# The last eight steps of FF2: the squares of a finished pair of tiles made one step later, behind GpSimd's second weight sum

## The chip, the cores and the metric

One core of one Trainium2 chip runs the whole kernel. The metric is the device time of one execution in microseconds (us). The kernel before takes 2620.69 us, the median of 3 runs (2619.88 to 2621.56).

Engines are named as in the profile: PE (TensorE, matmuls), DVE (VectorE), ACT (ScalarE), POOL (GpSimd), SP (the queue that issues most DMAs). L199 is line 199 of the kernel.

## The reference, cut to what matters

The kernel computes one layer of an encoder for 640 tokens of width 2048. The change lies in its last part, the down projection of the feed-forward block and the final norm:

```
x = x + (silu(h @ w_gate) * (h @ w_up)) @ w_down        # h = RMSNorm(x); w_down is 5632 x 2048
y = x * rsqrt(mean(x * x, axis=-1) + 1e-6) * norm_final
```

The mean of squares is taken over all 2048 columns of x, so every finished output tile of the down projection (128 columns by 640 tokens) gives its squares to one running sum.

## The kernel before

FF2, the down projection, runs as 32 steps. A step takes one pair q of output tiles (columns q and q + 8 of the 16 tiles) and some 5 or 6 blocks of the inner dimension; pair q has steps q, q + 8, q + 16 and q + 24, so that the last eight steps (24 to 31) each finish a pair. Each step multiplies 2 x 2 blocks with seven products instead of eight. The products run in the order p1, p6, p7, p2, p5, p4, p3 (`quartet`, L916), and with five blocks each is 15 matmuls of 128x128 by 128x320: for each block one with the weight's high half and the activation's high half (L207), one with the high half and the low half (L208), and one with the weight's low half (L209). Steps 30 and 31 are cut in two: an early part (p1, p6, p7, p5, p4) of both and then a late part (p2, p3).

Around a product stand these instructions:

- SP loads four weight blocks for a step (L936: b12, b22, b11, b21, in this order). They go through six buffers, and a load waits until its buffer's last reader is done. The load of b22 for the next step takes the buffer of this step's b12, which p7's weight split reads last.
- DVE makes b12 - b22 (L949) and s6 = b11 - that (L951) for the next step, in the middle of this one.
- POOL makes b22 - s6 into b11 (L954, the weights of p5) and b21 - s6 into b21 (L963, the weights of p4). L963 overwrites what p2 reads, so it waits for p2's split.
- ACT writes the high half of a product's weights (L198) and DVE the low half (L199), both 128x640. The pair of buffers is that of the product three before.
- DVE adds each finished product from PSUM to the tiles of the pair (L973, 128x320); after p6, in the last eight steps, three more adds read SBUF alone.
- POOL loads the activations of a coming step (L980).

The engines work in the order in which a scheduler has put their instructions; a wait at the head of one holds all that stands behind it on that engine.

The squares: `add_square` (L274) has ACT square a tile of 128x640 (L280; L277 for the very first, which starts the sum) and POOL add it to the running sum `ssq` (L281). In the kernel before, the loop over steps 0 to 29 calls it after the whole of a step t >= 24, twice, for the two tiles of the pair. The functions `squares` and `finish` do the same for the last two pairs and write the output; they are not changed. `n.later` is a list of stretches of the program; `keep_behind` (L155) ties each ACT, DVE and POOL instruction of such a stretch to the instruction of its engine that was emitted last ahead of the stretch, so that the scheduler cannot pull it forward past that one.

Of the kernel before, what the change touches and what calls it, by code (L numbers as in the profile page):

```python
# [29 lines left out]
STEPS = 32  # L30
# [3 lines left out]
def active(step):  # L34

    return [j for j in range(NPAIR) if (step - START[j]) % STEPS < 8]
# [13 lines left out]
class Net:  # L50
# [20 lines left out]
    def add(self, queue, work):  # L71
        self.queues.setdefault(queue, []).append(work)
# [230 lines left out]
def build(nc, tc, io, pools):  # L303
    n = Net(nc, tc, io, pools)
# [526 lines left out]
    r_b, ssq = n.get("S"), n.get("S")  # L831
# [169 lines left out]
    def fetch_late():  # L1001
        for which in late:
            for j in active(0):
                if j not in raw_pairs:
                    fetch(j, which)
        late.clear()

    def split_raws():
        at = n.emitted()
        which, own = raws.pop(0)  # L1010
        for j, k, raw in own:
            for a in range(k):
                t = n.get("S")
                hi, lo = hl = pack(t, HT)
                part = raw[:, a * HT:a * HT + HT]
                nc.scalar.activation(hi, part, AF.Identity)
                (nc.vector, nc.gpsimd)[a].tensor_tensor(lo, part, f(hi), ALU.subtract)
                lefts[j + a][which] = t, hl
            n.put("S", raw)
        n.later.append((at, n.emitted()))  # L1020

    def keep_last(which):

        at = n.emitted()
        t = n.get("S")
        hi, lo = hl = pack(t, HT)
        nc.scalar.activation(hi, kept[which], AF.Identity)  # L1027
        (nc.vector, nc.gpsimd)[which % 2].tensor_tensor(lo, kept.pop(which), f(hi), ALU.subtract)
        lefts[NPAIR - 1][which] = t, hl
        if not kept:  # L1030
            n.put("S", *kept_own)
        n.later.append((at, n.emitted()))
# [83 lines left out]
    def fetch_waiting(left):  # L1116
        while len(waiting) > left:
            for j, which in waiting.pop(0):
                fetch(j, which)

    def step(t, part="all"):
        now = active(t)
        nxt = active(t + 1) if t + 1 < STEPS else []
        cnt, q, last = len(now), t % 8, t >= STEPS - 8

        def after(which):
            gone = [j for j in now if j not in nxt]
            n.put("S", *(lefts[j][which][0] for j in gone))
            if t == 0:
                fetch_late()  # L1130
                if which in (1, 2):
                    split_raws()
                for x in {0: (0,), 2: (1,), 4: (2,), 3: (4,), 5: (3,), 6: (5, 6)}.get(which, ()):
                    keep_last(x)
            waiting.append([(j, which) for j in nxt if j not in now and j != NPAIR - 1])
            fetch_waiting(2)

        if t < 8:
            x, y = n.get("S"), n.get("S")
            dma(out=x, in_=x2_d[q])  # L1140
            dma(out=y, in_=x2_d[q + 8])
            sums.append((x, y, n.get("S") if q % 2 == 0 else sums[-1][2]))
        x, y, u = sums[q]
        c11, c21, c12, c22 = x[:, :HT], x[:, HT:], y[:, :HT], y[:, HT:]
        us = u[:, HT * (q % 2):HT * (q % 2) + HT]
        o = 2 * sum(len(active(i)) for i in range(q, t, 8))
        load = lambda z: io["w_down"][q + 8 * (z % 2), :, o + cnt * (z // 2):o + cnt * (z // 2) + cnt]
        for name, bank in quartet(cnt, load, [lefts[j] for j in now], None, after, part):
            if name == "p1":
                if t < 8:  # L1150
                    nc.scalar.activation(us, bank, AF.Identity)
                else:
                    add(us, us, bank)
                add(c11, c11, bank)
            elif name == "p6":
                add(us, us, bank)
                if last:
                    for c in (c21, c22, c12):
                        add(c, c, us)
            elif name == "p7":  # L1160
                add(c21, c21, bank)
                add(c22, c22, bank)
            elif name == "p5":
                add(c22, c22, bank)
                add(c12, c12, bank)
            elif name == "p2":
                add(c11, c11, bank)
            elif name == "p4":
                add(c21, c21, bank)
            elif name == "p3":  # L1170
                add(c12, c12, bank)
            yield name

    def run(*args):
        for _ in step(*args):
            pass

    for t in range(STEPS - 2):
        run(t)
        if t >= STEPS - 8:  # L1180
            if t == STEPS - 8:
                ssq = n.get("S")
            for i in range(2):
                n.add_square(ssq, sums[t % 8][i], t == STEPS - 8 and i == 0, "S")


    r_y = n.get("S")

    def squares(q, half):
        h = slice(half * HT, half * HT + HT)  # L1190
        t = n.get("S")
        for i in range(2):
            nc.scalar.activation(t[:, i * HT:i * HT + HT], sums[q][i][:, h], AF.Square)
        if q == 6:
            for i in range(2):
                nc.vector.tensor_tensor(ssq[:, h], ssq[:, h], t[:, i * HT:i * HT + HT], ALU.add)
        n.put("S", t)
        return n.rstd_steps({half: [ssq[:, h], t[:, :HT], t[:, HT:]]}, D, None) if q == 7 else None
# [10 lines left out]
                nc.vector.scalar_tensor_tensor(t, t, gain, n.spread[half], ALU.mult, ALU.mult)  # L1209
            (nc.scalar if half == 0 and i % 2 else nc.sync).dma_start(out=io["o_y"][:, m, h], in_=t)  # L1210

    run(STEPS - 2, "early")
    squares(6, 1)
    run(STEPS - 1, "early")
    norm = squares(7, 1)
# [10 lines left out]
    at = n.emitted()  # L1226
# [99 lines left out]
```

## Time and profile before

| what | us |
|---|---|
| median of 3 runs | 2620.69 |
| the profiled execution | 2621.49 |
| its span, first to last instruction | 2619.7 |
| PE busy in the span | 2565.2 |
| DVE busy in the span | 2027.7 |
| POOL busy in the span | 663.8 |

The profiled execution is 0.8 us above the median of the runs. The times of single instructions below count from the start of the span. Steps 25 to 29, in which the kernel makes squares beside full steps, lie between 2482 and 2567 us.

### The profile page before, as it was taken

Reading aid. Unit: us, or ns where it says so; the run is one execution under the profiler, and the core shown is the slowest. Engines: PE = TensorE matmul, PEld = TensorE weight load, DVE = VectorE, ACT = ScalarE, POOL = GpSimd, SP = SyncE. Lnnn points to the kernel's source line nnn. Section 1 sums busy time; section 2 is a strip of 40 time slices with the busy share of each in tenths; the row PEclk is TensorE's granted clock in tenths of the full one; section 3 lists DMA queues with packets and bytes.
Section 4 is the critical chain, followed back from the end, with each engine's and each line's share of the span. In section 5 each row is a group of like instructions: output and inputs, shape, how many; then the busy total and the mean of one; then the engine's idle time right before and its main releaser. Section 6 shows DMA issues by size and latency. Waiting matters only on the chain.

```text
span 2619.7 us, 45100 instructions
## 1 busy us (share of the span) xinstructions
PE 2565.2 (98%) x17437; PEld 2527.9 (96%) x17437; DVE 2027.7 (77%) x3133; ACT 1101.9 (42%) x1797; POOL 663.8 (25%) x573
## 2 busy tenths in 40 slices
PE   8999999999999999999999999999999899999997
PEld 8999998999899999999999999999999899999996
DVE  5775676766866888788888888888888877777797
ACT  5553444444633644443433333433434333333343
POOL 0000000000301203332333333323324433333353
PEclk9999999999999999999999999999999999999998
DMA  5322232444655433443343343343445865666655
GB/s 172 101 69 91 94 102 86 133 124 130 214 188 185 155 131 122 160 162 126 131 142 126 130 144 123 131 146 120 133 147 176 280 189 157 175 175 169 192 156 176
DMA packets 178678, 383.87 MB, mean 147 GB/s; under 512 B 21856, under 2 KB 74080, under 8 KB 178464
## 3 DMA queue, kind: packets, MB, share of 16 engines
q1 hardware_dynamic: 154128, 326.92, 38.8%
q0 software_dynamic: 23184, 52.77, 7.1%
q8 instruction: 137, 2.24, 0.3%
q10 hardware_dynamic: 1152, 1.31, 0.1%
q14 instruction: 77, 0.63, 0.1%
HBM read 299.61 MB, written 80.58 MB: 145 GB/s over the span
## 4 chain that ended last, share of the span: by engine, by line
PE 85%; DVE 8%; DMA 3%; ACT 2%; issue 2%; POOL 0%; SPq 0%; DVEq 0%; ACTq 0%; POOLq 0%
PE dn L209 18%; PE dn L207 18%; PE dn L208 18%; PE at L207 9%; PE at L208 9%; PE at L209 9%; DVE W L199 2%; PE at L324 2%; DMA W<-w_down 1%; PE at L419 1%; DVE S L973 1%; ACT W L198 1%; PE at L215 1%; PE at L214 1%; ACT S L440 0%
## 5 line engine op out<-in xcount | busy, mean ns | idle before, releaser
L207 PE MATMUL dn<-S,W 128*128 128x320 f32 x3694 | 1152.5, 312 | 5.2 <-ACT S L1027 2.7
L209 PE MATMUL dn<-S,W 128*128 128x320 f32 x3694 | 1144.5, 310 | 6.7 <-DVE W L199 6.3
L208 PE MATMUL dn<-S,W 128*128 128x320 f32 x3694 | 1143.3, 310 | 2.0 <-DVE S L203 1.7
L198 ACT ACTIVATE W<-W 128x1024 fp32r<-128x1024 f32 (+2 forms) x632 | 608.2, 963 | 965.9 <-PE dn L208 542.8
L199 DVE TENSOR_TENSOR W<-W,W 128x1024 fp32r<-128x1024 f32 (+2 forms) x632 | 738.7, 1169 | 81.5 <-ACT W L198 77.6
L209 PEld LDWEIGHTS dn<-S,W 128*128 128x128 f32 x3694 | 694.1, 188 | 10.5 <-DVE W L199 10.1
L207 PEld LDWEIGHTS dn<-S,W 128*128 128x128 f32 x3694 | 694.7, 188 | 9.0 <-ACT S L1027 3.0
L208 PEld LDWEIGHTS dn<-S,W 128*128 128x128 f32 x3694 | 694.4, 188 | 4.1 <-DVE S L203 1.9
L209 PE MATMUL at<-S,W 128*128 128x320 f32 x1594 | 493.5, 310 | 4.9 <-DVE W L199 4.8
L207 PE MATMUL at<-S,W 128*128 128x320 f32 x1594 | 492.8, 309 | 0.5 <-ACT W L198 0.5
L208 PE MATMUL at<-S,W 128*128 128x320 f32 x1594 | 492.5, 309 | 0.0
L954 POOL TENSOR_TENSOR W<-W,W 128x1024 f32<-128x1024 f32 (+2 forms) x75 | 158.9, 2118 | 637.5 <-DVE W L199 453.6
L209 PEld LDWEIGHTS at<-S,W 128*128 128x128 f32 x1594 | 299.2, 188 | 7.3 <-DVE W L199 7.3
L207 PEld LDWEIGHTS at<-S,W 128*128 128x128 f32 x1594 | 299.3, 188 | 0.8 <-ACT W L198 0.8
L208 PEld LDWEIGHTS at<-S,W 128*128 128x128 f32 x1594 | 299.3, 188 | 0.0
L973 DVE TENSOR_TENSOR S<-S,dn 128x320 f32<-128x320 f32 x358 | 163.8, 480 | 65.4 <-PE dn L209 65.0
L963 POOL TENSOR_TENSOR W<-W,W 128x1024 f32<-128x1024 f32 (+2 forms) x75 | 163.6, 2181 | 118.9 <-DVE W L199 113.5
L949 DVE TENSOR_TENSOR W<-W,W 128x1024 f32<-128x1024 f32 (+2 forms) x76 | 124.6, 1640 | 62.8 <-DMA W<-w_down 29.5
L973 DVE TENSOR_TENSOR S<-S,at 128x320 f32<-128x320 f32 x262 | 123.3, 480 | 51.4 <-PE at L209 50.5
L980 POOL DMA_DIRECT2D S<-act_d x161 | 88.0, 547 | 178.6 <-PE dn L209 92.0
L951 DVE TENSOR_TENSOR W<-W,W 128x1024 f32<-128x1024 f32 (+2 forms) x76 | 83.4, 1097 | 61.6 <-DMA W<-w_up 31.4
L1044 DVE TENSOR_TENSOR S<-S,half 128x320 fp32r<-128x320 f32 x147 | 120.0, 837 | 1.9
(162 smaller groups left out, 2223.3 us busy)
## 6 DMA issues: line engine op xcount, KB each, us to landing
S<-act_d POOLq DMA_DIRECT2D x161, 320.0 KB, 3.7
W<-w_gate SPq DMA_DIRECT2D x88, 512.0 KB
W<-w_up SPq DMA_DIRECT2D x88, 512.0 KB
W<-w_in SPq DMA_DIRECT2D x66, 512.0 KB
W<-w_down SPq DMA_DIRECT2D x64, 384.0 KB
act_d<-half SPq DMA_DIRECT2D x147, 160.0 KB
act_d<-S SPq DMA_DIRECT2D x147, 160.0 KB
W<-w_down SPq DMA_DIRECT2D x68, 320.0 KB
```

The costliest lines, as they stand in the source:

```text
L198: self.nc.scalar.activation(hi, src, AF.Identity)
L199: self.nc.vector.tensor_tensor(lo, src, f(hi), ALU.subtract)
L207: mm(out, a[0], b[0], start=first, stop=False)
L208: mm(out, a[0], b[1], start=False, stop=False)
L209: mm(out, a[1], b[0], start=False, stop=last)
L949: nc.vector.tensor_tensor(b12[:, w], b12[:, w], b22[:, w], sub)
L951: nc.vector.tensor_tensor(s6[:, w], b11[:, w], b12[:, w], sub)
L954: eng.tensor_tensor(b11[:, w], b22[:, w], s6[:, w], sub)
L963: eng.tensor_tensor(b21[:, w], b21[:, w], s6[:, w], sub)
L973: add = lambda o, a, b: nc.vector.tensor_tensor(o, a, b, ALU.add)
L980: nc.gpsimd.dma_start(out=r(sh(t, 2, HT)), in_=r(act_d[which, :, j]))
L1044: nc.vector.tensor_tensor(r(src), src, hi, ALU.subtract)
```

## The change

The call of `add_square` moves from the end of step t into step t + 1, to the place where the generator of that step has just handed over product p5; `late_squares` also marks the stretch in `n.later`. For step 29 the place is p5 of the early part of step 30. The sums, their order and the tiles are the same.

```
+    ssq = None
+
+    def late_squares(t):
+
+        nonlocal ssq
         if t >= STEPS - 8:
             if t == STEPS - 8:
                 ssq = n.get("S")
+            at = n.emitted()
             for i in range(2):
                 n.add_square(ssq, sums[t % 8][i], t == STEPS - 8 and i == 0, "S")
+            n.later.append((at, n.emitted()))
+
+    for t in range(STEPS - 2):
+        for name in step(t):
+            if name == "p5":
+                late_squares(t - 1)
...
-    run(STEPS - 2, "early")
+    for name in step(STEPS - 2, "early"):
+        if name == "p5":
+            late_squares(STEPS - 3)
```

On DVE, PE and SP the order of the instructions stays as it was. On POOL and ACT it changes. The rows below are from step 28, in which the squares of step 27's pair are made; steps 26, 27 and 29 are alike but for the places of single loads L980. Names are buffers: W weights, S activations and tiles, numbers tell them apart.

POOL before, from the first weight sum of step 28 (L954) to that of step 29:

```order
L954 TENSOR_TENSOR W_4121_27114<-W_4120_27112,W_4122_27117 128x640
L281 TENSOR_TENSOR S_4023_26565<-S_4023_26565,S_4115_27102 128x640
L980 DMA S_4163_27384<-act_d 128x640
L980 DMA S_4166_27407<-act_d 128x640
L281 TENSOR_TENSOR S_4023_26565<-S_4023_26565,S_4116_27105 128x640
L980 DMA S_4170_27431<-act_d 128x640
L963 TENSOR_TENSOR W_4132_27190<-W_4132_27190,W_4122_27117 128x640
L954 TENSOR_TENSOR W_4149_27288<-W_4148_27286,W_4150_27291 128x640
```

POOL now, the same stretch:

```order
L954 TENSOR_TENSOR W_4119_27108<-W_4118_27106,W_4120_27111 128x640
L963 TENSOR_TENSOR W_4130_27184<-W_4130_27184,W_4120_27111 128x640
L281 TENSOR_TENSOR S_4044_26692<-S_4044_26692,S_4136_27229 128x640
L281 TENSOR_TENSOR S_4044_26692<-S_4044_26692,S_4137_27232 128x640
L980 DMA S_4170_27431<-act_d 128x640
L954 TENSOR_TENSOR W_4147_27282<-W_4146_27280,W_4148_27285 128x640
```

Both sums of squares (L281) have moved from between the two weight sums to behind the second one (L963).

ACT before, from the split of p1's weights in step 28 to that of p4's (the rows L198 are p1, p6, p7, p2, p5, p4):

```order
L198 ACTIVATE W_4123_27119<-W_4121_27114 128x640
L198 ACTIVATE W_4126_27143<-W_4122_27117 128x640
L280 ACTIVATE S_4115_27102<-S_3371_22438 128x640
L198 ACTIVATE W_4130_27169<-W_4119_27110 128x640
L280 ACTIVATE S_4116_27105<-S_3372_22439 128x640
L198 ACTIVATE W_4134_27193<-W_4132_27190 128x640
L198 ACTIVATE W_4136_27214<-W_4121_27114 128x640
L198 ACTIVATE W_4139_27236<-W_4132_27190 128x640
```

ACT now, the same stretch:

```order
L198 ACTIVATE W_4121_27113<-W_4119_27108 128x640
L198 ACTIVATE W_4124_27137<-W_4120_27111 128x640
L198 ACTIVATE W_4128_27163<-W_4117_27104 128x640
L198 ACTIVATE W_4132_27187<-W_4130_27184 128x640
L198 ACTIVATE W_4134_27208<-W_4119_27108 128x640
L280 ACTIVATE S_4136_27229<-S_3371_22438 128x640
L280 ACTIVATE S_4137_27232<-S_3372_22439 128x640
L198 ACTIVATE W_4139_27236<-W_4130_27184 128x640
```

The two squares (L280) have moved from ahead of p7's and p2's splits to behind p5's split and ahead of p4's.

## Rows read from the trace of the kernel before

**Rows 1.** PE's waits from 2484 to 2590: total us, times, longest us.

```profile
PE dn L209 <- DVE W L199: 4.9, 5, 1.8
PE at L209 <- DVE W L199: 1.7, 5, 0.6
```

**Rows 2.** Stretches from p7 to p7: length, busy PE, PEld, DVE, ACT, POOL, PEclk, DMA, GB/s.

```profile
2486.60:2502.00 15.40, 15.40 (x107) 15.40 (x106) 14.48 (x22) 7.55 (x11) 6.99 (x5) 1.00 0.36 91
2502.00:2518.00 16.00, 15.72 (x108) 15.41 (x106) 14.64 (x22) 7.46 (x11) 9.38 (x12) 1.00 0.76 223
2518.00:2534.70 16.70, 15.98 (x108) 15.46 (x107) 15.23 (x24) 6.43 (x9) 9.37 (x10) 1.00 0.60 161
2534.70:2551.50 16.80, 15.83 (x106) 15.31 (x105) 15.27 (x22) 7.42 (x11) 8.06 (x7) 1.00 0.45 134
2551.50:2569.40 17.90, 15.94 (x107) 15.41 (x106) 15.11 (x23) 7.43 (x11) 9.29 (x9) 1.00 0.63 170
```

**Rows 3.** Chain that ended last, 2484 to 2590: start, us, what.

```profile
2533.91 4.04 DMA W<-w_down
...
2550.82 5.14 DMA W<-w_down
...
2574.86 5.12 DMA W<-w_down
2580.18 2.63 POOL W L963
```

**Rows 4.** Timeline of DVE, 2519 to 2541: start, us, group [idle before <-releaser].

```profile
2521.23 0.87 DVE L949 TENSOR_TENSOR W<-W,W 128x640 f32<-128x640 f32 x1 [1.47 <-DMA W<-w_down]
...
2522.42 0.81 DVE L199 TENSOR_TENSOR W<-W,W 128x640 fp32r<-128x640 f32 x1
2523.16 1.28 DVE L973 TENSOR_TENSOR S<-S,S 128x320 f32<-128x320 f32 x3
...
2525.16 0.82 DVE L199 TENSOR_TENSOR W<-W,W 128x640 fp32r<-128x640 f32 x1
...
2529.69 2.07 DVE L199 TENSOR_TENSOR W<-W,W 128x640 fp32r<-128x640 f32 x1
2531.68 0.47 DVE L973 TENSOR_TENSOR S<-S,dn 128x320 f32<-128x320 f32 x1
2532.08 1.80 DVE L199 TENSOR_TENSOR W<-W,W 128x640 fp32r<-128x640 f32 x1
...
2537.98 1.03 DVE L949 TENSOR_TENSOR W<-W,W 128x640 f32<-128x640 f32 x1 [1.44 <-DMA W<-w_down]
```

**Rows 5.** Timeline of POOL, the same stretch.

```profile
2529.51 1.57 POOL L954 TENSOR_TENSOR W<-W,W 128x640 f32<-128x640 f32 x1 [1.35 <-DVE W L199]
2531.05 2.15 POOL L281 TENSOR_TENSOR S<-S,S 128x640 f32<-128x640 f32 x1
...
2534.26 1.59 POOL L281 TENSOR_TENSOR S<-S,S 128x640 f32<-128x640 f32 x1
...
2536.74 1.58 POOL L963 TENSOR_TENSOR W<-W,W 128x640 f32<-128x640 f32 x1
```

**Rows 6.** Timeline of ACT, 2500 to 2506 and 2519 to 2541.

```profile
2502.13 0.74 ACT L198 ACTIVATE W<-W 128x640 fp32r<-128x640 f32 x1 [1.52 <-PE dn L208]
...
2529.80 0.74 ACT L280 ACTIVATE S<-S 128x640 f32<-128x640 f32 x1 [0.91 <-DVE S L973]
```

**Rows 7.** Timelines of DVE and POOL elsewhere: 824 to 832, 1500 to 1506.

```profile
823.82 5.84 DVE L203 SCALAR_TENSOR_TENSOR S<-S,gains,S 128x640 fp32r<-128x640 f32 x3 [0.52 <-ACT S L202]
...
823.15 7.94 POOL L281 TENSOR_TENSOR S<-S,S 128x640 f32<-128x640 f32 x4 [25.57 <-ACT S L280]
...
1501.61 3.10 DVE L1044 TENSOR_TENSOR S<-S,half 128x320 fp32r<-128x320 f32 x2
...
1501.76 2.60 POOL L963 TENSOR_TENSOR W<-W,W 128x1024 f32<-128x1024 f32 x1 [1.56 <-DVE W L199]
```

**Rows 8.** Timeline of DVE, 2554 to 2575.

```profile
2572.88 0.82 DVE L949 TENSOR_TENSOR W<-W,W 128x640 f32<-128x640 f32 x1 [2.04 <-DMA W<-w_down]
```

More of the change, by code (lines that the diff above doesn't have):

```diff
@@ L1176, in run @@
             pass
-    for t in range(STEPS - 2):
-        run(t)
+    ssq = None
+    def late_squares(t):
+        nonlocal ssq
         if t >= STEPS - 8:
```

## The prediction

> **What bounds the kernel now.** I read the waits of PE first, in the steps that the change touches: from 2484 to 2590 PE waits 6.6 us, ten times, always for the low half of a product's weights that DVE makes (L199) [rows 1]. That is all that a change here can win. The stretches from one p7 to the next show what a step pays: a step of five blocks has 105 matmuls and takes 15.4 us where PE never waits (the first stretch, granted clock 1.00); steps 26 to 29 take 16.0, 16.7, 16.8 and 17.9, which is 0.6 + 1.3 + 1.4 + 2.5 = 5.8 us over [rows 2]. Step 25, before any pair of square sums, has no wait.
>
> Then the chain that ended last: it doesn't run through PE there but round a loop of DVE and a weight load. L949 of a step waits for the load of b22 (it stands idle 1.44 to 1.47 us before it) [rows 4]; DVE then works without a pause from L949 to the low half of the next p7 (2521.23 to 2533.88, 12.65 us); that split frees the buffer for the next load, issued at 2533.91, 4.04 us [rows 3], and the next L949 starts at 2537.98 [rows 4]. One turn is 16.75 us, against PE's 15.4.
>
> What lengthens the turn is POOL. A low half alone takes 0.81 us; the one at 2529.69 takes 2.07 and ends 0.68 after POOL's L954 (2529.51 + 1.57 = 2531.08), the one at 2532.08 takes 1.80 and ends 0.68 after the sum L281 (2531.05 + 2.15 = 2533.20) [rows 4, 5]. The sum in turn starts only when the first of these ends, 2531.76, and ends 1.44 later. So a POOL sum and a DVE instruction with two SBUF inputs go one after the other, whoever comes first; when both have more to do they alternate: elsewhere four L281 took 7.94 and three L203 between them 5.84, 1.95 to 1.99 each [rows 7]. The small adds obey too: two L1044 of 128x320 took 3.10 us around one POOL sum, while three free adds of that size take 1.28 [rows 4, 7]. An add from PSUM (2531.68, 0.47 us) does not wait, though a sum is running [rows 4, 5].
>
> **What it removes.** In before the first L281 holds up p7's low half by 1.80 - 0.81 = 1.0 us, inside the turn. The second (2534.26) meets only p2's low half, which ends before the load has landed, so it costs the turn next to nothing. Without both, the turn is 11.65 + 4.1 = 15.7 us, nearly PE's own. The squares on ACT ahead of p7's split go as well; ACT is half idle, so moving them costs nothing there, as long as p4's high half is ready in time (below).
>
> **What it adds.** I count from T, the start of p7 on PE. ACT splits p5 at T + 0.1 (L198 released by the end of p6) [rows 6] for 0.74; then the squares follow, 0.74 each [rows 6], done at 1.6 and 2.4. p4's high half comes at about 3 and is needed at 6.6: hidden. On POOL, L963 waits for p2's low half and fills 0 to 1.55; the sums queue behind it. The load of b22 lands at about 2.2: p7's low half ended 0.8 us ahead of T in before (2533.88 against 2534.7 [rows 2, 4]) and now ends 1.8 ahead, by what was removed; 4.0 on top.
>
> - First sum: 1.7 to 3.25. L949 is ready at 2.2 and gets its turn after it: done at 3.25 + 0.7 = 3.95, as if it had started at 3.1.
> - Second sum: ready since 3.25, takes its turn behind L949, done 1.44 later, 5.4. p5's low half, ready at 4.25, is held to 5.4 + 0.7 = 6.1 instead of 5.1: 1.0 us lost.
> - In before p4's low half ends 4.7 after L949's start (2521.23 to 2525.98, less 0.05 by which L949 was stretched) [rows 4]. Now: 3.1 + 4.7 + 1.0 = 8.8.
> - PE wants p5's low half at 4.7 and p4's at 6.9 (two products of 2.2, three of 2.2, and two matmuls of 0.15). It waits 1.4 at p5 and 0.5 at p4, and each restart costs 0.1: 2.15 us a step.
>
> If L949 came before the first sum, the second would meet the three S,S adds instead, and p4's half would end at the same 8.8. Both sums now lie in the stretch in which DVE has no pause, and the way PE - ACT - POOL - DVE - PE is longer than a step can hide. DMAs: the loads L980 that stand between the sums read buffers that PE has already left; each takes POOL 0.55 us. SP's queue isn't passed by anything.
>
> **The sum.** Step 25 (one sum only, held against the three adds): 0.5. Step 26, where an L980 stands ahead of the first sum, which pushes it to 2.1: 2.5. Steps 27 and 28: 2.15 each. Step 29, whose b22 took 5.14 [rows 3]: between 2.15 and 2.5, say 2.3. Together 9.6 against 5.8: +3.8. In step 30 L949 now starts at 3.5 after T [rows 8] in a gap of POOL; both sums then stand in front of it (1.7 to 4.8), which holds it 1.3 us; p4's half, the load that it releases (2574.86) and L963 behind that load, the end of the chain [rows 3], shift with it: +1.3. In all +5.1 us: 2621.49, the profiled execution, becomes 2626.6. That execution lies 0.8 above the median of the runs, so against the median: 2625.8.
>
> **Bounds.** A sum costs at least nothing (in a pause or beside PSUM adds) and at most 1.57 + what alternation adds. With the load at 5.14 in every step and the L980 always between the sums, a step pays 2.5 and step 30 0.5 more: +7.5, 2628.2.
>
> **Rivals.** (1) Faster: the sums don't hold DVE. Then the turn is 15.7 us, PE pays 0.3 a step instead of 1.45, 4 x 1.15 = 4.6 is won, and p7's earlier split gives step 30 some 0.4: 2615.7. It decides if DVE's instructions at 2 to 6 us after T run at 0.81 beside a sum. Against it stand the stretched instructions of rows 4 and 7 [rows 4, 7]. The Trainium skill (Advanced Engine Details and Errata, VectorE Performance Modes) says that the port shared with GpSimd blocks VectorE's two-port modes, and lists no such mode for tensor_tensor; by that alone the time would be 2615.7. The trace differs, with 2.07 us for 0.81 in a tensor_tensor beside a POOL sum. (2) Even: DVE doesn't let POOL in between instructions that follow without a gap, so that the second sum slips to the two PSUM adds behind p7. Then p5 is 0.4 late, p4's half ends at 8.4, a step pays 1.6, step 30 0.7: 0.5 + 2.0 + 3 x 1.6 - 5.8 + 0.7 = +2.2, 2622.9. For it: DVE starts an instruction some 0.08 us before the last one ends (2531.68 against 2531.76 [rows 4]). Against it: the alternation of rows 7.
>
> **How the numbers follow.** Forecast 0.60 (2623.5 to 2628.2), even 0.27 (2620 to 2624), faster 0.13 (2614.5 to 2618.5). The measurement tells 0.2%, 5.2 us, from no change, so the forecast itself lies at that bound: I put 0.36 of it over 2625.9 and the rest below, with the even case: slower 0.36, same 0.52, faster 0.12. The range reaches from within the faster case to a little over the upper bound: 2616.5 to 2629.5.
>
> **What would show it.** In the changed profile: L281 twice right behind L963; L949 or p5's low half and the three adds at 1.4 to 2 us instead of 0.8 and 1.3; p7's low half at 0.81; PE's waits at p5 of 1.3 or more in steps 26 to 29, and stretches of about 17.5 us. If p5's low half stays at 0.81 and stretches are under 16, rival 1 is right; if the last sum lies beside p7's adds, rival 2. I would be wrong altogether if the weight load, not the sums, ends the wait of L949.

## The result, and the profile after

The changed kernel took 2626.57 us (median of 22 runs, 2622.61 to 2630.55), the kernel before 2622.52 beside it (22 runs, 2617.75 to 2626.61): a ratio of 1.0014, 95% interval 1.0008 to 1.0020. It is slower by some 4 us, and that is less than 0.2%. Each kernel was profiled twice. The profiled executions took 2627.99 and 2626.71 us after, 2621.49 and 2620.28 before. Two executions below, one of before (3562.64 us) and one of a variant (5075.77 us), were far slower than all others of their kernels, and the ratios leave them out.

The stretches of the changed kernel from one p7 to the next, steps 25 to 29, and behind them the way from p7 of step 30 to the first matmul of L251 (columns as in [rows 2], which show the same steps of before):

```profile
2488.00:2503.83 15.83, 15.66 (x107) 15.40 (x106) 15.13 (x22) 6.44 (x9) 6.25 (x7) 1.00 0.43 110
2503.83:2521.10 17.27, 15.66 (x107) 15.39 (x106) 15.47 (x22) 7.22 (x11) 10.46 (x11) 1.00 0.69 202
2521.10:2538.55 17.45, 15.93 (x107) 15.40 (x106) 14.79 (x22) 7.33 (x11) 8.65 (x10) 1.00 0.66 180
2538.55:2555.86 17.31, 15.93 (x108) 15.41 (x106) 15.10 (x22) 6.43 (x9) 7.89 (x7) 1.00 0.36 95
2555.86:2573.17 17.31, 15.94 (x108) 15.41 (x106) 13.86 (x21) 7.01 (x11) 11.54 (x10) 1.00 0.57 166
2573.17:2599.33 26.16, 22.84 (x138) 22.18 (x137) 20.59 (x34) 11.06 (x19) 8.90 (x8) 0.87 0.49 151
```

Steps 25 to 29 take 85.2 us where they took 82.8: +2.4. The last row answers to this one of before:

```profile
2569.42:2592.95 23.53, 20.85 (x138) 19.80 (x136) 19.91 (x35) 8.24 (x15) 9.45 (x9) 1.00 0.51 166
```

That is +2.6, and its granted clock is 0.87 where it was 1.00. So the 5.0 us between the two lie half in the steps and half in the tail; the second pair of profiles gives +2.6 and +2.5. PE's waits of the changed kernel, 2484 to 2600 (total us, times, longest us; the longest is at p4 of step 30), beside [rows 1]:

```profile
PE at L209 <- DVE W L199: 4.8, 6, 2.2
PE dn L209 <- DVE W L199: 4.6, 4, 1.2
```

Step 28 of the changed kernel starts its p7 at 2538.55. POOL's timeline there, beside [rows 5], and then DVE's, beside [rows 4]:

```profile
2538.37 1.59 POOL L963 TENSOR_TENSOR W<-W,W 128x640 f32<-128x640 f32 x1 [3.43 <-DVE W L199]
2540.09 3.69 POOL L281 TENSOR_TENSOR S<-S,S 128x640 f32<-128x640 f32 x2
```

```profile
2535.95 0.81 DVE L199 TENSOR_TENSOR W<-W,W 128x640 fp32r<-128x640 f32 x1
...
2540.51 1.85 DVE L949 TENSOR_TENSOR W<-W,W 128x640 f32<-128x640 f32 x1 [2.22 <-DMA W<-w_down]
2542.28 0.47 DVE L973 TENSOR_TENSOR S<-S,dn 128x320 f32<-128x320 f32 x1
2542.68 1.79 DVE L199 TENSOR_TENSOR W<-W,W 128x640 fp32r<-128x640 f32 x1
2544.39 1.28 DVE L973 TENSOR_TENSOR S<-S,S 128x320 f32<-128x320 f32 x3
2545.59 0.87 DVE L973 TENSOR_TENSOR S<-S,at 128x320 f32<-128x320 f32 x2
2546.39 0.81 DVE L199 TENSOR_TENSOR W<-W,W 128x640 fp32r<-128x640 f32 x1
```

p7's low half (2535.95) is free now, 0.81 us. Both sums stand behind L963. The first holds L949 (1.85 us for 0.8), the second holds p5's low half (2542.68, 1.79 for 0.81). The adds from PSUM keep their 0.47 and 0.87. Steps 27 and 29 are alike. In step 26 the load landed before the first sum, so L949 was free and the second sum met the three S,S adds (2.66 for 1.28):

```profile
2505.39 0.82 DVE L949 TENSOR_TENSOR W<-W,W 128x640 f32<-128x640 f32 x1 [1.82 <-DMA W<-w_down]
...
2506.53 1.80 DVE L199 TENSOR_TENSOR W<-W,W 128x640 fp32r<-128x640 f32 x1
2508.25 2.66 DVE L973 TENSOR_TENSOR S<-S,S 128x320 f32<-128x320 f32 x3
```

The tail runs through other pieces. Of the chain that ended last, step 29's end and step 30 (start, us, what), in the changed kernel:

```profile
2564.54 3.52 DMA W<-w_down
...
2570.45 2.16 POOL W L954
...
2573.53 4.68 DMA W<-w_down
```

The load at 2573.53 is the third of three that SP issues behind L954, and it is what the L949 in step 30 waits for; that one starts at 2578.23, 5.1 us after p7's start, where it was 3.5 before [rows 8]. p4's low half stands behind it and PE waits 2.2 us. In before the same load took 3.9 us:

```profile
2568.95 3.90 DMA W<-w_down
```

POOL ahead of that load, before and then in the changed kernel:

```profile
2564.31 1.57 POOL L963 TENSOR_TENSOR W<-W,W 128x640 f32<-128x640 f32 x1 [3.69 <-DVE W L199]
...
2566.43 1.59 POOL L954 TENSOR_TENSOR W<-W,W 128x640 f32<-128x640 f32 x1
```

```profile
2568.22 2.26 POOL L963 TENSOR_TENSOR W<-W,W 128x640 f32<-128x640 f32 x1 [3.82 <-DMA W<-w_down]
2570.45 2.15 POOL L954 TENSOR_TENSOR W<-W,W 128x640 f32<-128x640 f32 x1
2572.55 0.57 POOL L980 DMA_DIRECT2D S<-act_d  x1
```

The low half of p6 on DVE, before, and the low halves of p6 and p7 in the changed kernel:

```profile
2564.47 2.09 DVE L199 TENSOR_TENSOR W<-W,W 128x640 fp32r<-128x640 f32 x1
```

```profile
2568.23 0.81 DVE L199 TENSOR_TENSOR W<-W,W 128x640 fp32r<-128x640 f32 x1
...
2569.64 1.52 DVE L199 TENSOR_TENSOR W<-W,W 128x640 fp32r<-128x640 f32 x1 [0.19 <-ACT W L198]
```

In before L963 starts 0.16 us ahead of the low half of p6 and has its turn first. In the changed kernel the two start together, L963 loses the turn, and L954 loses one to the low half of p7: so L954 ends 0.6 us ahead of p7 on PE, where it ended 1.4 ahead. One fetch L980 is issued 1.0 us ahead of the load; before, none was.

### The profile page after: what moved, and what is told of

Read it like the earlier page. It is cut to its first block, busy times and chain, and to the rows that moved or that the text cites. A ratio compares the mean times of both kernels' runs of the same rounds, so it can differ in the third digit from the quotient of the medians.

```text
span 2626.2 us, 45095 instructions
## 1 busy us (share of the span) xinstructions
PE 2568.3 (98%) x17437; PEld 2531.8 (96%) x17437; DVE 2029.1 (77%) x3133; ACT 1100.8 (42%) x1797; POOL 663.2 (25%) x573
## 4 chain that ended last, share of the span: by engine, by line
PE 86%; DVE 7%; DMA 2%; ACT 2%; issue 2%; POOL 0%; SPq 0%; DVEq 0%; ACTq 0%; POOLq 0%
PE dn L209 18%; PE dn L207 18%; PE dn L208 18%; PE at L207 9%; PE at L208 9%; PE at L209 9%; DVE W L199 2%; PE at L324 2%; PE at L419 1%; DMA W<-w_down 1%; DVE S L973 1%; PE at L215 1%; PE at L214 1%; ACT W L198 0%; ACT S L440 0%
## 5 line engine op out<-in xcount | busy, mean ns | idle before, releaser
L198 ACT ACTIVATE W<-W 128x1024 fp32r<-128x1024 f32 (+2 forms) x632 | 608.5, 963 | 976.1 <-PE dn L208 556.4
L954 POOL TENSOR_TENSOR W<-W,W 128x1024 f32<-128x1024 f32 (+2 forms) x75 | 159.7, 2130 | 637.4 <-DVE W L199 440.3
L963 POOL TENSOR_TENSOR W<-W,W 128x1024 f32<-128x1024 f32 (+2 forms) x75 | 163.0, 2174 | 131.5 <-DVE W L199 121.9
L949 DVE TENSOR_TENSOR W<-W,W 128x1024 f32<-128x1024 f32 (+2 forms) x76 | 123.4, 1623 | 70.1 <-DMA W<-w_down 34.6
L980 POOL DMA_DIRECT2D S<-act_d x161 | 88.1, 548 | 169.4 <-PE dn L209 87.2
```

Source lines behind the costliest of these rows:

```text
L198: self.nc.scalar.activation(hi, src, AF.Identity)
L949: nc.vector.tensor_tensor(b12[:, w], b12[:, w], b22[:, w], sub)
L954: eng.tensor_tensor(b11[:, w], b22[:, w], s6[:, w], sub)
L963: eng.tensor_tensor(b21[:, w], b21[:, w], s6[:, w], sub)
L980: nc.gpsimd.dma_start(out=r(sh(t, 2, HT)), in_=r(act_d[which, :, j]))
```

## The experiments

Two things are asked: whether the sums cause the waits in steps 25 to 29, and what makes step 30 late.

"Before" and "after" name the two kernels; the ratios are to before, run beside each on the same chip (median 2624.0 us beside the first four kernels, 2622.3 beside the next three with rounds, 2623.5 beside the last three).

**Without the sums.** The squares stay, the sum L281 goes, in both kernels:

```
-                n.add_square(ssq, sums[t % 8][i], t == STEPS - 8 and i == 0, "S")
+                first = t == STEPS - 8 and i == 0
+                sq = ssq if first else n.get("S")
+                nc.scalar.activation(sq, sums[t % 8][i], AF.Square)
+                if not first:
+                    n.put("S", sq)
```

On after:

> The changed kernel without the eleven L281 sums on GpSimd of the last eight steps (the squares on ACT stay; the sum of squares is left out, so the output is not the reference's). Theory (a GpSimd sum and a VectorE instruction with two SBUF inputs take turns, and each sum costs DVE 1.0 to 1.9 us in the stretch in which it has no pause): DVE's turn falls from 17.3 to 11.65 + 4.05 = 15.7 us, PE pays about 0.3 us a step in place of 1.7 to 2.1, five steps: 4 x 1.5 and 1 to 2 in step 30, so 7 to 8 us under the changed kernel: 2618 to 2619 against 2626.5. L949 0.8 us, p5's low half 0.81. Rival A (what costs is that ACT's squares stand behind p5's split, or that L949 waits for its load): the time stays at 2625 to 2627.

On before:

> The kernel before without the eleven sums L281 (the squares stay at their old place; the sum is left out, so the output is not the reference's). Theory: the first sum holds p7's low half 1.0 us a step and the second costs nothing, so the turn goes from 16.75 to 15.7 us, as without the sums in the changed kernel; PE's 5.8 us in steps 26 to 29 become 1.2 to 2.2: 4 us under the kernel before, 2618 to 2619 against 2622.5, and within 1 us of the changed kernel without sums. Rival A: the two kernels without sums differ by the 4 us by which the kernels with sums differ.

After without sums took 2617.41 us, about as expected (ratio 0.9976, 0.9965 to 0.9986), before without sums 2622.96 (0.9996, 0.9987 to 1.0004). The windows of the first (steps 26 to 29 in one):

```profile
2501.57:2563.17 61.60, 61.60 (x422) 61.60 (x421) 52.07 (x88) 28.54 (x43) 24.73 (x27) 1.00 0.63 181
```

and of the second, steps 25 to 29 and the tail:

```profile
2486.30:2564.95 78.65, 77.78 (x528) 76.99 (x527) 68.14 (x109) 36.64 (x53) 28.49 (x33) 1.00 0.59 163
2564.95:2593.67 28.72, 24.06 (x137) 23.39 (x136) 20.55 (x35) 8.70 (x15) 4.79 (x5) 0.82 0.44 135
```

In after, four steps without sums take 4 x 15.40 us, with PE busy all the time: everything that steps 26 to 29 lost was the sums' doing. The time rival A gave for after, 2625 to 2627, is excluded. In before the five steps fell from 82.8 to 78.65 us, the 4 us expected; but its tail took 28.7 instead of 23.5 and gave all of it back. So the expectation for before was right in the steps and wrong in the total. Rival A's mark, a difference between the two kernels without sums, was there (5.6 us in the medians, 4.5 in the profiles). In the profiles 3.0 us of it lie in the tail, and 1.6 in steps 28 and 29 of before, where the load for step 28's L949 took 5.3 us. The tail's cause shows on POOL and in the chain of before without sums:

```profile
2563.49 1.63 POOL L980 DMA_DIRECT2D S<-act_d  x3
```

```profile
2564.48 6.13 DMA W<-w_down
```

Two fetches L980 are issued in the microsecond ahead of the load that L949 waits for and a third 0.1 us behind its start, and that load takes 6.1 us (3.9 in before). This is taken up below.

**L949 behind p4's low half.** L949 waits for a load, and p5's and p4's low halves, which PE wants soon, stand behind it on DVE. What it makes is wanted only for the second and third product of the next step. The edit orders it behind p4's low half, from step 25 on:

```
+    for t in range(STEPS - 7, STEPS):
...
+                low = dve(starts[t - 1][k], p4[t - 1][k])[-1]
+                tc.add_manual_dep(dve(starts[t][k], None)[0], low.name, info, reason="pin")
```

`dve(...)[0]` is the first instruction of step t on DVE, L949; `low` is the low half of p4 in the step ahead.

> The changed kernel with one order more: in steps 25 to 31 the first subtraction of a step on DVE (L949) stands behind the low half of the step before's p4, no longer ahead of p5's low half. Nothing is left out. Theory: the sums cost only because L949, which waits for the load of b22, stands in DVE's queue ahead of p5's and p4's low halves that PE wants soon; with L949 behind them (some 4 us after the start of p7, for work that PE wants 13 us after it) the turn of DVE and the load has about 2 us to spare, PE's waits in steps 26 to 29 fall from 7.3 to under 1 us, and the sums cost nothing wherever they stand: 2616 to 2619 against 2626.5. Rival B (the sums cost DVE time that it does not have, whatever the order): no more than 2 us won, 2624.5 to 2626.5.

> The kernel before with the same order of L949 behind p4's low half. Nothing is left out. Theory: 2616 to 2619 against 2622.5, within 1 us of the changed kernel with that order, since the sums' place no longer reaches PE. Rival B: 2621 to 2622.5, some 4 us under the changed kernel with that order.

Before with it took 2618.44 us (0.9979, 0.9969 to 0.9989), as expected. After with it took 2627.95 (1.0009, 1.0000 to 1.0018): the theory's number failed there, and the 9.5 us between the two failed its other mark, 1 us. DVE and POOL of that kernel at step 27:

```profile
2523.41 5.25 DVE L973 TENSOR_TENSOR S<-S,S 128x320 f32<-128x320 f32 x3
2528.59 0.81 DVE L199 TENSOR_TENSOR W<-W,W 128x640 fp32r<-128x640 f32 x1
```

```profile
2522.81 1.59 POOL L963 TENSOR_TENSOR W<-W,W 128x640 f32<-128x640 f32 x1
2524.36 1.83 POOL L281 TENSOR_TENSOR S<-S,S 128x640 f32<-128x640 f32 x1
...
2526.73 1.57 POOL L281 TENSOR_TENSOR S<-S,S 128x640 f32<-128x640 f32 x1
```

With L949 gone, the scheduler put the three S,S adds ahead of p5's low half. Each of the three lost its turn to one of POOL's three instructions, 5.25 us for 1.28, and p5's low half stood behind them. So a second edit moved those adds, too:

```
+            if which == 3 and last:
+                for c in (c21, c22, c12):
+                    add(c, c, us)
...
             elif name == "p6":
                 add(us, us, bank)
-                if last:
-                    for c in (c21, c22, c12):
-                        add(c, c, us)
```

The added lines run right behind the split of p5's weights.

> The changed kernel, nothing left out, with two orders more on DVE: L949 behind the low half of p4, and the three S,S adds no longer ahead of the low half of p5 (emitted behind its split). With L949 alone moved, those three adds stood ahead of p5's low half and took 4.7 to 5.3 us there, each behind one of GpSimd's L963 and two L281. Theory (a sum costs only where DVE has no time to spare before a low half that PE waits for): PE's waits in steps 26 to 29 fall under 0.5 us a step, 2616 to 2619 against 2626.5, the same within 1.5 us as the kernel before with these two orders. Rival B (the sums cost DVE time that it does not have): 2623 or more, 3 us or more over the kernel before with these two orders.

> The kernel before, nothing left out, with the same two orders on DVE. Theory: no wait of PE over 0.5 us in steps 26 to 29 (with L949 alone moved there were 0.9 and 0.7 at p5's low half in steps 27 and 28), 2616 to 2618 against 2622 to 2624, the lower of all the kernels that compute everything. Rival B: as with L949 alone, 2618.4 or more.

Before with both orders took 2616.70 us (0.9982, 0.9973 to 0.9991), after with both 2621.42 (0.9993, 0.9984 to 1.0002). PE's waits of after with both, 2480 to 2565:

```profile
PE dn L207 <- DVE S L973: 1.1, 3, 0.4
```

With L949 alone moved, steps 26 to 29 waited 6.5 us for low halves; now no such wait is listed, and 1.1 for adds. Steps 25 to 29 take 79.6 us, for 84.6 with L949 alone moved and 77.0 without sums. In the profiles the two kernels are 0.8 us apart (spans of 2615.7 and 2614.9), as the theory had it. The medians are 4.7 apart, and there the theory's two marks for after failed: 2616 to 2619, and 1.5 us from before with the two orders. The 3 us or more that rival B named came. After's profile is its fastest run (its eleven go from 2617.4 to 2623.9). What the slower runs lose no profile shows; this stays open. Before with L949 late, or with both orders, beats both kernels.

**Every sum twice.** In the changed kernel (`add_square` is written out in its place, of which this is the end):

```
                     nc.gpsimd.tensor_tensor(ssq, ssq, sq, ALU.add)
+                    nc.gpsimd.tensor_tensor(ssq, ssq, sq, ALU.add)
```

> The changed kernel with every sum made twice on GpSimd (the second adds the same squares again, so the output is not the reference's). Theory (GpSimd's sums and DVE's instructions with two SBUF inputs take turns, each sum holding one of them by up to 1.6 us): the two more sums of a step meet two of the three S,S adds, p4's low half comes 2.5 to 3.2 us later, PE's wait at p4 grows from 0.4 to about 3 us in steps 26 to 29 and by 1 to 1.5 in step 25: 2636 to 2642. Rival F (the sums give way to DVE while it has no pause, and slip into the adds from PSUM): 2626.5 to 2630.

It took 2644.59 us (1.0080, 1.0067 to 1.0094). DVE's three S,S adds in step 27 of it:

```profile
2533.10 5.73 DVE L973 TENSOR_TENSOR S<-S,S 128x320 f32<-128x320 f32 x3
```

As the theory had it, the added sums meet these adds; PE's waits at p4 grew to 3.4 to 4.7 us. Steps 25 to 29 took 106.4 us, 21.2 more for nine added sums. In that stretch 65 matmuls stand 0.267 us apart, not 0.147; that is 7.8 us. The other 13.4 are 1.5 a sum. The half clock is why it came out over the expected 2642: it begins behind a wait, as in this window (granted clock 0.54):

```profile
2540.30:2544.00 3.70, 3.58 (x14) 3.59 (x15) 3.46 (x7) 0.00 (x0) 0.68 (x2) 0.54 0.83 244
```

Rival F is excluded.

**Only the sums moved.** The squares on ACT stay where they were in before:

```
     def late_squares(t):
...
+        while made:
+            sq = made.pop(0)
+            nc.gpsimd.tensor_tensor(ssq, ssq, sq, ALU.add)
+            n.put("S", sq)
...
             if name == "p5":
                 late_squares(t - 1)
+        if t >= STEPS - 8:
+            make_squares(t)
```

> The changed kernel with the squares on ACT (L280) back at their old place, right behind the adds that finish a tile, ahead of p7's split; only the sums on GpSimd are at the new place, behind L963. Nothing is left out. Theory (only the place of the sums counts; ACT is half idle): 2625.5 to 2627.5, as the changed kernel; PE's waits of steps 26 to 29 1.3 to 1.8 and 0.4 a step. Rival E (the squares behind p5's split cost, too): 1 us or more faster than 2626.5. Squares that are ready earlier can let the first sum start 0.3 to 0.4 us earlier where L963 ends early; that changes p5's wait by as much at most.

2623.55 us (1.0003, 0.9994 to 1.0012), 3 under the changed kernel's 2626.5. That is rival E's mark. But the variant didn't hold its place: with the squares ready early, the scheduler put the sums of three of the five pairs ahead of L963 again. Of steps 26 to 29, only in step 28 both stand behind it, as POOL and that step's window show:

```profile
2533.05 1.57 POOL L963 TENSOR_TENSOR W<-W,W 128x640 f32<-128x640 f32 x1 [2.91 <-DVE W L199]
2534.59 3.69 POOL L1198 TENSOR_TENSOR S<-S,S 128x640 f32<-128x640 f32 x2
```

```profile
2533.16:2550.35 17.19, 15.93 (x107) 15.40 (x106) 15.17 (x22) 7.38 (x11) 10.93 (x9) 1.00 0.38 109
```

17.19 against 17.31 of the changed kernel: in this one step the squares' place is worth 0.1 us. As a test of the whole it is inconclusive, and rival E is not settled by the time.

**Step 30 without its squares.** Does the sum hold L949 in step 30? The edit drops one call, and a second kernel puts GpSimd work that reads nothing in its place:

```
     for name in step(STEPS - 2, "early"):
         if name == "p5":
-            late_squares(STEPS - 3)
+            at = n.emitted()
+            for k in (3, 2):
+                sq = n.get("S")
+                nc.scalar.activation(sq, sums[0][0], AF.Square)
+                for _ in range(k):
+                    nc.gpsimd.memset(sq, 0.0)
+                n.put("S", sq)
+            n.later.append((at, n.emitted()))
```

The first kernel has the line with - only, the second the lines with + as well.

> The changed kernel without the squares and sums of step 29's pair, which it makes in step 30 (they are left out, so the output is not the reference's). Forecast (the two sums hold L949 in step 30 by 1.3 us): PE's wait at p4 of step 30 falls from 2.2 to about 1, the way from p7 of step 30 to the first L251 from 26.2 to 24.9, the time by 1.3 to 2625.2. Rival C (L949 of step 30 comes late through its load, which waits for p5's split, L954, L963 and the load of b21, not through the sums): the wait stays at 2.0 to 2.4 and the time at 2626 to 2627.

> The changed kernel without the squares and sums of step 29's pair (the output is not the reference's); in their place, in step 30, GpSimd runs five MEMSETs of an unused tile (0.63 us each for 80x640 elsewhere in the trace of before, so 3.1 us), which read nothing from SBUF and stand in GpSimd's queue where the two sums stood, ahead of the act_d fetches L980. Theory D (without the two sums, three L980 are issued in the same microsecond as the load that L949 of step 30 waits for, and that load took 7.1 us in place of 4.7; the sums had kept the fetches back): with the MEMSETs in front the fetches come 3 us later, the load takes 4.5 to 5.5 us, PE's wait at p4 of step 30 is 2 to 2.8 us in place of 4.6, 2626 to 2628. Rival (the load is slow for another reason): the wait stays over 4 us and the time at 2629 to 2631.

Without the two sums the kernel got slower: 2630.11 us (1.0029, 1.0018 to 1.0039), with a wait of 4.6 us at p4 of step 30 for 2.2. Both expected times were wrong, the forecast's and rival C's. C's reading, that L949 is late through its load, is what the trace shows, but the load didn't stay as it was. POOL, DVE and the chain of it:

```profile
2573.01 1.10 POOL L980 DMA_DIRECT2D S<-act_d  x2
```

```profile
2581.09 0.82 DVE L949 TENSOR_TENSOR W<-W,W 128x640 f32<-128x640 f32 x1 [6.40 <-DMA W<-w_down]
```

```profile
2573.98 7.08 DMA W<-w_down
```

The load takes 7.1 us, not 4.7. A fetch behind the sums in POOL's queue was kept back by them (in the changed kernel the next L980 behind the one at 2572.55 start at 2577.33, four of them, when that load has nearly landed). Without the sums two L980, not one, are issued in the microsecond ahead of the load, and a third 2.3 us behind it. Theory D, above, speaks of three in the same microsecond; it was two. The second kernel, POOL, DVE, chain:

```profile
2570.36 2.92 POOL L1229 MEMSET S<- 128x640 f32 x5 [1.02 <-ACT S L1227]
2573.23 1.59 POOL L980 DMA_DIRECT2D S<-act_d  x3
```

```profile
2570.23 0.81 DVE L199 TENSOR_TENSOR W<-W,W 128x640 fp32r<-128x640 f32 x1
2574.43 0.83 DVE L949 TENSOR_TENSOR W<-W,W 128x640 f32<-128x640 f32 x1 [3.39 <-DMA W<-w_down]
```

```profile
2569.76 4.65 DMA W<-w_down
```

With the MEMSETs in front, one fetch alone goes ahead of the load again, the load takes 4.65 us, and PE's wait at p4 is 1.4: theory D holds. That the wait is even under the changed kernel's 2.2, with a load as long, is L954's doing: it ended 1.4 us ahead of p7 here. Part of it was lost again one product on (a wait of 3.1 us in step 31), so that the tail takes 26.4 us (27.9 without the MEMSETs), and the time is 2627.55 (1.0020, 1.0011 to 1.0029). The Trainium skill (DMA: Bandwidth & Descriptors, Issuing engines are not separate DMA queues) says that DMAs started by any engine run on the same 16 engines and interleave; the runs agree, with 7.08 us for the load behind two fetches and 4.65 behind one. A by-product: the low half at 2570.23 takes its 0.81 us, and the MEMSET that starts beside it 0.13 us later, and has no input, takes 0.63 like the four behind it; neither holds the other.

**The two kernels again,** with no edit.

> The kernel before, unchanged, profiled a second time. In the profiles of the changed kernel and of four variants TensorE's matmuls run 0.267 us apart (half clock) for 5 to 11 us in step 30 or 31 and for 3 to 5 us near 2050 us; in the one profile of the kernel before they do not. If that belongs to the kernel before, it is absent again, and the time is 2620 to 2622. If it comes and goes with the run, one or both stretches are there, and the time is 1.4 to 4 us longer, 2622 to 2626, with the waits of steps 26 to 29 as before (0.6, 0.6 + 0.4, 0.8 + 0.4, 1.8 + 0.4).

> The changed kernel, unchanged, profiled a second time. In its first profile TensorE's matmuls ran 0.267 us apart (half clock) from 2580 to 2588 us in step 30 and 31, behind a wait of 2.2 us at p4; in both profiles of the kernel before they did not, with waits of 0.6 to 1.0 and 1.8 us there. If that belongs to the changed kernel, the stretch is there again (some 5 to 8 us long, 2 to 3 us lost) and the way from p7 of step 30 to the first L251 is 26 us or more (23.5 to 23.7 in before). If it came by chance, it is 23.5 to 24.5. The waits of steps 26 to 29 are as in the first profile: 1.8, then 1.3 to 1.4 and 0.4 a step, the stretches 17.3 to 17.5 us from step 26 on.

Before took 2620.28 us, after 2626.71. Before had the waits expected, and after nearly: its step 26 lost 2.3 us (1.9 in the first profile) and its step 28 1.7, where the load landed ahead of the first sum and p4 alone waited. The tail was 23.5 us in before, without half clock, and 26.0 in after, with it from 2584.5 to 2587.9. One expectation for before failed: the stretch at half clock near 2050 us was there, and the time was not 1.4 to 4 us longer but 1.2 shorter.

## Why the prediction was right, and where it was not

- **Order and mechanism in steps 25 to 29: right.** DVE and POOL take turns where the forecast put them; in step 26 (in the second profile in step 28) the load lands ahead of the first sum, the other case that it named. Without the sums the four steps have no wait (61.60 us), and each added sum costs 1.5 us. Rival 1 (the sums don't hold DVE) would have shown 0.81 at L949 and p5's low half. With it falls the rule of the Trainium skill named there (Advanced Engine Details and Errata, VectorE Performance Modes) as far as it would leave a tensor_tensor free: 1.85 us for 0.82. Rival 2 (the second sum slips) would have shown p5's low half at 0.81; it took 1.79 in each of steps 27 to 29.
- **A step's price: right within 0.4 us.** From p7's start, step 28: load landed 2.0 (forecast 2.2), p5's low half 5.9 (6.1), p4's 8.7 (8.8), PE's loss 1.3 at p5 and 0.4 at p4 (1.4 and 0.5). In total 1.9 to 2.05 a step for 2.15 (in the second profile 1.7 to 2.05).
- **The terms that were mis-sized:** step 26 lost 1.87 in the first profile for 2.5 (there the first sum began at 1.9 and L949 was free; the second profile has 17.72, 2.3 lost), and step 29 1.91 for 2.3, since its load took 3.8 us, not the 5.1 taken over from before. In before it took 5.1 in both profiles; why stays open. The steps came to +2.4 (second pair +2.6), the forecast said +3.8.
- **The step that failed: step 30.** The forecast was that both sums hold L949 by 1.3 us there. They end at 2577.39, and L949 starts at 2578.23, free, 0.82 us. It was late through its load: L954 ended 1.4 us ahead of p7 before and 0.6 ahead after, since L963 and L954 each lost a turn to a low half, and the load behind it took 4.7 us for 3.9, with a fetch ahead of it; 0.8 and 0.8 are the 1.6 us by which PE's wait at p4 grew. For the half clock in the tail the forecast had no term. Taking the sums away made it worse. That 5.1 was forecast for the total and 5.0 and 5.1 came in the profiles is the work of two errors that cancel, -1.3 in the steps and +1.3 in the tail.
- **Profile and medians.** The medians differ by 4.0 us, the profiles by 6.5 and 6.4. In both pairs 1.4 to 1.6 us of that lies ahead of the change: step 25's p7 starts later in after. It is a difference between runs: 1.2 and 1.35 of it are there 1000 us after the start, where the two kernels are the same. The stretch at half clock near 2050 us does not account for it. Of the fourteen profiles taken of these kernels and variants only the first of before lacks that stretch, but its lead is the same on both sides of it: the matmul that it starts at 2040 us comes 0.83 us later in the first profile of after, and the one at 2060 us 0.85 later. Of the forecast's +5.1, then, the profiles show 5.0 and 5.1 behind the change, and the medians 4.0 in all; the 1 us between them stays open.

## What to carry to other kernels

Here a sum that is "hidden" on GpSimd was paid by VectorE wherever both read two tiles of SBUF, so ask at which of VectorE's instructions it will land and whether that engine has a pause there. The larger gain, some 5 us in before, was in the order of the waiting engine: an instruction that waits for a load, and whose result is wanted late, should stand behind the ones that are ready and wanted soon. Work on a queue also keeps back the DMAs behind it; when it is moved or removed, see which load those DMAs will now run beside.

## What the runs showed of the hardware that was not expected

- **Turns are strict, one instruction each:** three S,S adds, 1.28 us when free, took 5.25 us beside three POOL instructions and 5.73 in the kernel with double sums. Beside MEMSETs, which read nothing, a low half kept its 0.81 us and the MEMSET its 0.63. The Trainium skill (SBUF — State Buffer, SBUF: two separate sides) has a lock between a VectorE instruction with two SBUF inputs and a GpSimd one that reads SBUF; the runs agree in both directions, with these numbers.
- **What is issued ahead of a load sets its time in step 30.** In eleven profiles L949 waits there for a load of 320 KB that is the third of three within a microsecond. With no fetch of act_d issued in that microsecond it took 3.9 to 4.2 us (both profiles of before, and the kernel with only the sums moved), with one 4.65 to 4.8 (six profiles), with two 6.1 and 7.1. Fetches behind it show no such cost: in after without sums four followed within 2.9 us, and it took 4.8. This does not cover every load: the 5.1 us in step 29 of before had one fetch ahead of it, and 3.8 in after, with one as well.
- **The half clock in the tail.** In the changed kernel the matmuls stand 0.267 us apart for some microseconds of step 30 and 31:

```profile
2580.00:2590.00 10.00, 8.65 (x40) 8.26 (x41) 9.96 (x17) 2.94 (x5) 3.64 (x2) 0.66 0.42 132
```

That is the 1.2 GHz level, behind a wait of 2.2 us at p4. It was there in both profiles of after, in neither of before, and also in both kernels without sums, in both with L949 alone late, in both with step 30 changed, and in the one with every sum twice; not in the two with both orders, though one of those waited 1.5 and 2.4 us there, nor in the one with only the sums moved (1.5 and 1.8 us). Wherever it came, PE had waited 1.8 us or more in steps 30 and 31; but before, too, waited 1.8 there and kept its clock. So the waits there don't decide it alone, and what does stays open. It is part of what the tail lost. Of the +2.6 us, 1.6 is the wait at p4. Some 20 matmuls at 0.12 us more are an estimated 2.4, and the waits behind p4's, which became shorter, gave some 1.4 back.
